# A hybrid attention block on one core: which column groups start with one k-tile, and when normalised queries and keys are scaled

## The chip, the cores and the metric

The kernel runs on one core of a Trainium2 chip. The metric is the time of one execution in microseconds of device time; 574.02 us is the median of three runs of the kernel before. The profile and its trace come from one further execution.

## What is computed

One decoder layer on x of 256 x 2048 in float32:

```python
mod = silu(c) @ w_ada + b_ada                  # 2048 -> 6144: shift, scale, gate
h = rms_norm(x, g_norm) * (1 + scale) + shift
proj = h @ w_in                                # 2048 -> 9296: q, k, v, z of groups a and b, and an indexer
# group a: 8 heads of 128, keys chosen by the indexer's 64 best scores; group b: 8 heads, causal
# q and k of each head are rms-normed; scores get ALiBi; y = attention * silu(z)
out = x + gate * (concat(ya, yb) @ w_out)      # 2048 -> 2048
```

## The kernel before

**Tiles.** `h` is kept transposed, as 16 k-tiles of 128 rows by 256 tokens. w_in has 19 column groups: q, k, v and z of the four quads b0, b1, a0, a1 (512 columns each, four heads), and three indexer groups i0, i1, i2. Float32 accuracy comes from splitting: ScalarE rounds a weight piece to `wh` (L322), VectorE subtracts to get `wl` (L332), and TensorE makes three matmuls for each k-tile and token half (L774 to L776). A *piece* is at most two k-tiles of one group, so 12 matmuls. There are 192 pieces, of which 160 belong to w_in.

**Loads.** All weights come through one in-order queue (SyncE), issued six loads ahead of the casts. w_ada is read transposed in 1 MB loads, two for each k-tile (shift `sh`, scale `sc`); VectorE reduces each against silu(c) (L289, called a *gemv* here). When both loads of the k-tiles of a chunk are reduced, `build_h` makes the h of that chunk (L402 to L418). Chunk 0 is k-tile 0, chunk 1 is k-tile 1, then chunks of two. A planner written in Python lists the loads. It walks the column groups in a fixed order and gives each as many k-tiles as are known then; `between()` inserts w_ada loads by the count of k-tiles listed so far. Where only k-tile 0 is known, the four groups z, q, k, v of a quad are loaded as one quad load of four pieces with one k-tile each. In the kernel before, the list begins: sh0, half of sc0, quad b1, the rest of sc0, then sh1, sc1, sh2, sc2 at once, then quad a0 (again k-tile 0 alone), za1 with k-tiles 0 and 1, sh3, qa1, ka1, va1, sc3, the indexer groups, and so on. Raw weights lie in a pool of four buffers; w_ada loads named by `EARLY` lie in a pool of two (`rawe`). A load waits in the queue until its buffer is free.

**Accumulation.** A group accumulates its listed k-tiles in PSUM; then an evacuation copies (L675) or adds (L677) the sum into SBUF. There are 55 evacuations of w_in groups.

**Attention beside the projections.** Python generators put out the attention work one step at a time, one step after each piece. `yield n` makes a generator skip n steps. `prep` takes the squares of a finished q or k group on ScalarE (L506), gets 1/rms on GpSimd in two instructions (`rsqrt`, L149 and L150), and after `yield 1` scales the eight 128 x 128 blocks on ScalarE (L513). The indexer runs in eight pairs: TensorE transposes q (`ptq`, L466), ScalarE copies it (`qi`, L468), TensorE makes logits (`lg`, L474 and L475), ScalarE applies relu (L477), VectorE adds to the scores (L479). A head transposes q and k (L531), scales k by `gneg` (L534), has GpSimd multiply the distances by the head's slope into `nb` (L536), makes scores (L540, L541), and VectorE adds `nb` and takes the extreme (L545); exp, transposes, value matmuls and the gate follow. The final order of groups is i2, i0, i1, then z, q, k, v of b0, b1, a0, a1. A piece of w_out that needs a head not yet put out forces that head's steps at once.

**Order on the engines.** A scheduler at build time orders each engine's instructions: among those that are ready by its own estimate of times it takes the one that was put out first. On the chip each engine follows that order.

Of the kernel before, what the change touches and what calls it, by code (L numbers as in the profile page):

```python
# [8 lines left out]
F32 = mybir.dt.float32  # L9
F32R = mybir.dt.float32r  # L10
AF = mybir.ActivationFunctionType
ALU = mybir.AluOpType

P = 128
L = 256
D = 2048
KT = D // P
DIN = 9296
HD = 128
# [19 lines left out]
CHUNKS = list(zip(EDGES, EDGES[1:]))  # L39
NC = len(CHUNKS)  # L40


ADA_AT, ADA_FIRST, ADA_GAP, ADA_LAG, GATE_AT, GATE_GAP = 4, 4, 5.5, 2, 150, 8


EARLY = {1, 2} | set(range(5, 2 * KT + KT * KT))


NO_WAIT = mybir.DependencyInfo(mybir.DependencyClass.NoSync, mybir.DependencyReason.DATA)
# [3 lines left out]
def hybrid_block(ctx: ExitStack, tc: tile.TileContext, x, cols, w_ada_t, w_in, w_out, out):  # L53
    nc = tc.nc
    consts = ctx.enter_context(tc.tile_pool(name="consts", bufs=1))
    hp = ctx.enter_context(tc.tile_pool(name="hp", bufs=27))
    up = ctx.enter_context(tc.tile_pool(name="up", bufs=37))
    rawp = ctx.enter_context(tc.tile_pool(name="rawp", bufs=4))
# [4 lines left out]
    rawe = early.enter_context(tc.tile_pool(name="rawe", bufs=2))  # L63
    late_pool = []

    def late_tiles():
        if not late_pool:
            early.close()
            late_pool.append(ctx.enter_context(tc.tile_pool(name="late", bufs=2)))
        return late_pool[0]  # L70
# [9 lines left out]
    def mm_tile(name):  # L80
        return psum.tile([P, 512], F32, tag="mm", bufs=4, name=name)
# [18 lines left out]
    cc = consts.tile([P, 85], F32, name="cc")  # L100
# [10 lines left out]
    dist = consts.tile([P, 384], F32, name="dist")  # L111
# [7 lines left out]
    dista = consts.tile([P, 384], F32, name="dista")  # L119
# [10 lines left out]
    for n in range(4):  # L130
        pt = mm_tile(f"pts{n}")
# [5 lines left out]
    for k0, k1 in CHUNKS:  # L137
        one = bmod[:, k0 + k1:2 * k1]
        nc.gpsimd.tensor_scalar(one, one, 1.0, None, op0=ALU.add)
    gneg = {}  # L140
    for i, g in enumerate("ab"):
        gt = consts.tile([P, 1], F32, name=f"gneg{g}")
        nc.vector.scalar_tensor_tensor(gt, cc[:, 64 + 2 * i:65 + 2 * i], -(HD ** -0.5),
                                       cc[:, 65 + 2 * i:66 + 2 * i], op0=ALU.mult, op1=ALU.mult)
        gneg[g] = gt

    def rsqrt(dst, ssq, n):
# [26 lines left out]
    ada = [ld for c in range(1, NC) for ld in ada_loads(c)]  # L174
# [2 lines left out]
        gates[4 * n + 3]["end"] = NC + n  # L177
    known, ready = CHUNKS[0][1], []
    pos = {g: 0 for g in ORDER}
    n_kt, ada_at, gate_at = 0, ADA_AT, GATE_AT  # L180

    def between():

        nonlocal ada_at, gate_at
        if ada and n_kt >= ada_at:
            for _ in range(ADA_FIRST if ada_at == ADA_AT else 1):
                ld = ada.pop(0)
                loads.append(ld)
                if "end" in ld:
                    ready.append((n_kt + ADA_LAG, CHUNKS[ld["end"]][1]))  # L190
            ada_at += ADA_GAP
        elif gates and n_kt >= gate_at:
            loads.append(gates.pop(0))
            gate_at += GATE_GAP

    turn = list(ORDER)
    while turn:
        while ready and (ready[0][0] <= n_kt or known == pos[turn[0]]):
            known = ready.pop(0)[1]
            if known == KT:  # L200
                turn.sort(key=FINAL.index)
        g = turn.pop(0)
        c0, w = COLS[g]
        seg0, end = pos[g], known
        assert end > seg0
        gs = [c + g[1:] for c in "zqkv"]
        if g[0] == "z" and end == seg0 + 1 and [pos[o] for o in gs] == 4 * [seg0]:

            between()
            turn = [o for o in turn if o not in gs]  # L210
            members = [w_load(w_in_r, o, COLS[o][0], 512, [seg0], "h", True, True, seg0 == 0, end == KT)
                       for o in gs]
            loads.append(dict(kind="quad", quad=g[1:], k=seg0, members=members))
            n_kt += 4
            for o in gs:
                pos[o] = end
                if end < KT:
                    turn.append(o)
            continue
        for k in range(seg0, end, 4):  # L220
            n = min(4, end - k)
            between()
            loads.append(w_load(w_in_r, g, c0, w, list(range(k, k + n)), "h", k == seg0, k + n == end,
                                seg0 == 0, end == KT))
            n_kt += n * w / 512
        pos[g] = end
        if end < KT:
            turn.append(g)
# [9 lines left out]
    n_start = 2 * CHUNKS[0][1] + 1  # L238
    loads.insert(n_start - 1, loads.pop(n_start))
    n_issued = 0  # L240
    late = []

    def issue(upto):
        nonlocal n_issued
        while n_issued < min(upto, len(loads)):
            ld = loads[n_issued]

            pool = rawe if ld["kind"] == "ada" and ld["to"][0] == "mod" and n_issued - n_start in EARLY else rawp
            raw = pool.tile([P, 2048], F32, tag="raw", name=f"raw{n_issued}")
            if ld["kind"] == "ada":  # L250
                h0, h1 = ld["h"]
                ld["v"] = raw[:, :h1 - h0]
                nc.sync.dma_start(ld["v"], w_ada_t[ld["col"] * P:(ld["col"] + 1) * P, h0:h1])
                while late:
                    nc.sync.dma_start(*late.pop(0))
            elif ld["kind"] == "quad":

                q, k = ld["quad"], ld["k"]
                base, off = 0 if q[0] == "a" else COLS["qb0"][0], 512 * int(q[1])
                v = raw.rearrange("p (c n) -> p c n", n=512)  # L260
                src = w_in[k * P:(k + 1) * P, base:base + 4096].rearrange("p (c n) -> p c n", n=1024)
                first_c = (COLS[ld["members"][0]["g"]][0] - base - off) // 1024
                if n_issued == n_start - 1:

                    nc.sync.dma_start(v[:, first_c:first_c + 1, :], src[:, first_c:first_c + 1, off:off + 512])
                    rest = [(lo, hi) for lo, hi in ((first_c + 1, 4), (0, first_c)) if hi > lo]
                    late.extend((v[:, lo:hi, :], src[:, lo:hi, off:off + 512]) for lo, hi in rest)
                else:
                    nc.sync.dma_start(v, src[:, :, off:off + 512])
                for m in ld["members"]:  # L270
                    c = (COLS[m["g"]][0] - base - off) // 1024
                    m["v"] = v[:, c:c + 1, :]
            else:
                kts, w = ld["kts"], ld["w"]
                v = raw[:, :len(kts) * w].rearrange("p (k n) -> p k n", n=w)
                nc.sync.dma_start(v, ld["src"][:, kts[0]:kts[-1] + 1, ld["c0"]:ld["c0"] + w])
                ld["v"] = v
            n_issued += 1

    mod = {}  # L280
# [219 lines left out]
    def prep(q, c):  # L500

        ssq = quad.setdefault((q, c), work.tile([P, 16], F32, name=f"ss{c}{q}", tag="ss", bufs=3))
        for t in range(2):
            for h in range(4):
                junk = work.tile([P, P], F32, name=f"j{c}{q}{t}{h}", tag="junk")
                nc.scalar.activation(junk, proj[c + q, t][:, h * HD:(h + 1) * HD], AF.Square,  # L506
                                     accum_out=ssq[:, 4 * t + h:4 * t + h + 1])
        rsqrt(ssq[:, 8:16], ssq[:, 0:8], HD)
        yield 1
        for t in range(2):  # L510
            for h in range(4):
                s = proj[c + q, t][:, h * HD:(h + 1) * HD]
                nc.scalar.activation(s, s, AF.Copy, scale=ssq[:, 8 + 4 * t + h:9 + 4 * t + h])  # L513
        yield 0
# [9 lines left out]
    def head(q, h):  # L524
        hs = slice(h * HD, (h + 1) * HD)
        hid = int(q[1]) * 4 + h
        name = f"{q}{h}"
        pt = ps_tile("tr", "tr" + name)
        for i, c in enumerate("qk"):
            for t in range(2):  # L530
                nc.tensor.transpose(pt[:, i * L + t * P:i * L + (t + 1) * P], proj[c + q, t][:, hs], ident)  # L531
        qk = late_tiles().tile([P, 512], F32, name="qk" + name, tag="qk", bufs=2)
        nc.vector.tensor_copy(qk[:, :L], pt[:, :L])
        nc.scalar.activation(qk[:, L:], pt[:, L:], AF.Copy, scale=gneg[q[0]])  # L534
        nb = late_tiles().tile([P, 384], F32, name="nb" + name, tag="nb", bufs=2)
        nc.gpsimd.tensor_scalar(nb, dista if q[0] == "a" else dist, 2.0 ** -(hid + 1), 0.0,  # L536
                                op0=ALU.mult, op1=ALU.add)
        yield 1
        ps = ps_tile("s", "s" + name)
        nc.tensor.matmul(ps[:, :P], qk[:, :P], qk[:, L:L + P], start=True, stop=True)  # L540
        nc.tensor.matmul(ps[:, P:384], qk[:, P:L], qk[:, L:], start=True, stop=True)  # L541
        ns = late_tiles().tile([P, 384], F32, name="ns" + name, tag="at", bufs=4)
        st = work.tile([P, 8], F32, name="st" + name, tag="st", bufs=4)
        for t, lo, hi in ((0, 0, P), (1, P, 384)):
            nc.vector.tensor_tensor_reduce(out=ns[:, lo:hi], in0=ps[:, lo:hi], in1=nb[:, lo:hi], scale=1.0,  # L545
                                           scalar=3e38, op0=ALU.add, op1=ALU.min, accum_out=st[:, t:t + 1])
        for t, lo, hi in ((0, 0, P), (1, P, 384)):
            nc.scalar.activation(ns[:, lo:hi], ns[:, lo:hi], AF.Exp, bias=st[:, t:t + 1], scale=-1.0,
# [174 lines left out]
    for j in range(total):  # L723
        sb = subs[j]
        ld = sb["ld"]
# [25 lines left out]
        g = ld["g"]  # L751
# [13 lines left out]
        for i, k, t in order:  # L765
            ps = acc_ps[g, t][:, :w]
# [51 lines left out]
```

## Time and profile before

| | us |
|---|---|
| median of 3 runs | 574.02 (574.01 to 574.69) |
| profiled execution, its own time | 578.7 |
| span of the profiled execution (first to last instruction) | 576.9 |
| TensorE busy | 553.6 (96% of the span) |
| VectorE busy | 444.5 (77%) |
| ScalarE busy | 319.6 (55%) |
| GpSimd busy | 48.0 (8%) |
| mean granted TensorE clock | 0.995 of full speed |

Ends of matmuls are modelled, so busy TensorE time hides short gaps; the distance between starts of consecutive matmuls shows them.

### The profile page before, as it was taken

What the parts mean: (1) busy time and instruction counts of PE and PEld (TensorE: products, weight loads), DVE (VectorE), ACT (ScalarE), POOL (GpSimd) and SP (SyncE); (2) the same over time, 40 slices, a digit from 0 to 9 for tenths busy, and PEclk for the clock granted to TensorE, in tenths of its full rate; (3) what the DMA queues carried; (4) which work ended last, traced back from release to release, by engine and by line L of the source; (5) the groups of instructions that cost most, each with busy time, mean ns of one, the idle gap of its engine ahead of it and who ended that gap; (6) DMA issues with size and microseconds to landing.
All of it is one profiled execution on the core that took longest, in us unless ns stands there. A gap on an engine that the chain in (4) does not pass through costs nothing.

```text
span 576.9 us, 7456 instructions
## 1 busy us (share of the span) xinstructions
PE 553.6 (96%) x2658; PEld 462.7 (80%) x2658; DVE 444.5 (77%) x683; ACT 319.6 (55%) x652; POOL 48.0 (8%) x62
## 2 busy tenths in 40 slices
PE   3889999999999999999799999999999999999996
PEld 2769888888889988976577888888888888887885
DVE  4877789898898898998689996678787576458452
ACT  4588563544444353576555566646776785554340
POOL 4100000000000000102201002111110210000000
PEclk9999999999999999999989999999999999999999
DMA  8999998898898987877845376767675468445611
GB/s 293 412 350 370 361 346 326 330 360 285 314 359 318 366 326 270 268 298 279 303 152 177 129 275 235 273 221 265 226 255 201 148 231 279 146 150 190 244 37 38
DMA packets 59670, 150.09 MB, mean 260 GB/s; under 512 B 3056, under 2 KB 9456, under 8 KB 53616
## 3 DMA queue, kind: packets, MB, share of 16 engines
q1 hardware_dynamic: 58480, 147.51, 71.1%
q10 hardware_dynamic: 1152, 2.10, 1.2%
q8 instruction: 21, 0.34, 0.2%
q14 instruction: 17, 0.14, 0.1%
HBM read 147.50 MB, written 2.10 MB: 259 GB/s over the span
## 4 chain that ended last, share of the span: by engine, by line
PE 87%; ACT 4%; DVE 2%; POOL 2%; issue 2%; DMA 1%; SPq 0%; DVEq 0%; ACTq 0%
PE mm_y_o L774 5%; PE mm_y_o L776 5%; PE mm_y_o L775 5%; PE mm_h_zb L776 3%; PE mm_h_zb L774 3%; PE mm_h_zb L775 3%; PE mm_h_za L775 3%; PE mm_h_i L776 3%; PE mm_h_i L775 3%; PE mm_h_i L774 3%; PE mm_h_qb L774 3%; PE mm_h_za L776 3%; PE mm_h_qb L776 3%; PE mm_h_qb L775 3%; PE mm_h_qa L774 3%; PE mm_h_ka L775 2%
## 5 line engine op out<-in xcount | busy, mean ns | idle before, releaser
L322 ACT ACTIVATE wh<-raw 128x1024 fp32r<-128x1024 f32 (+3 forms) x192 | 188.2, 990 | 140.5 <-PE mm_y_o L776 32.9
L332 DVE TENSOR_TENSOR wl<-raw,wh 128x1024 fp32r<-128x1024 f32 (+3 forms) x192 | 215.0, 1140 | 60.5 <-ACT wh L322 59.9
L289 DVE CUSTOM_DVE_ANT_0 raw<-raw,s_row 128x2048 f32<-128x2048 f32 (+1 forms) x49 | 110.2, 2250 | 14.1 <-DMA raw<-in_w_ada_t 14.1
L774 PE MATMUL mm_y_o<-wh,yT 128*128 128x512 f32 x128 | 51.7, 404 | 0.0
L775 PE MATMUL mm_y_o<-wl,yT 128*128 128x512 f32 x128 | 49.9, 390 | 0.0
L776 PE MATMUL mm_y_o<-wh,yT 128*128 128x512 f32 x128 | 49.8, 390 | 0.0
L774 PE MATMUL mm_h_i<-wh,hhi 128*128 128x384 f32 (+1 forms) x96 | 31.7, 330 | 0.0
L775 PE MATMUL mm_h_i<-wl,hhi 128*128 128x384 f32 (+1 forms) x96 | 31.5, 328 | 0.0
L536 POOL TENSOR_SCALAR nbb<-dist 128x384 f32<-128x384 f32 x8 | 8.0, 1001 | 283.3 <-DVE mmod L289 211.2
L776 PE MATMUL mm_h_i<-wh,hlo 128*128 128x384 f32 (+1 forms) x96 | 31.4, 329 | 0.0
L776 PEld LDWEIGHTS mm_y_o<-wh,yT 128*128 128x128 f32 x128 | 24.0, 188 | 5.4 <-DVE yT L575 0.2
L774 PEld LDWEIGHTS mm_y_o<-wh,yT 128*128 128x128 f32 x128 | 24.1, 188 | 4.7 <-ACT yT L574 0.2
L775 PEld LDWEIGHTS mm_y_o<-wl,yT 128*128 128x128 f32 x128 | 24.1, 188 | 4.6
L774 PE MATMUL mm_h_qa<-wh,hhi 128*128 128x512 f32 x64 | 25.6, 409 | 0.9 <-ACT wh L322 0.9
L774 PE MATMUL mm_h_zb<-wh,hhi 128*128 128x512 f32 x64 | 26.4, 412 | 0.0
L774 PE MATMUL mm_h_vb<-wh,hhi 128*128 128x512 f32 x64 | 26.4, 412 | 0.0
L775 PE MATMUL mm_h_za<-wl,hhi 128*128 128x512 f32 x64 | 25.1, 392 | 0.9 <-DVE wl L332 0.9
L774 PE MATMUL mm_h_kb<-wh,hhi 128*128 128x512 f32 x64 | 25.7, 405 | 0.0
L775 PE MATMUL mm_h_zb<-wl,hhi 128*128 128x512 f32 x64 | 25.7, 401 | 0.0
L775 PE MATMUL mm_h_vb<-wl,hhi 128*128 128x512 f32 x64 | 25.6, 400 | 0.0
L774 PE MATMUL mm_h_qb<-wh,hhi 128*128 128x512 f32 x64 | 25.5, 401 | 0.0
L774 PE MATMUL mm_h_za<-wh,hhi 128*128 128x512 f32 x64 | 25.5, 406 | 0.0
(216 smaller groups left out, 1227.3 us busy)
## 6 DMA issues: line engine op xcount, KB each, us to landing
raw<-in_w_in SPq DMA_DIRECT2D x51, 1024.0 KB, 5.9
raw<-in_w_ada_t SPq DMA_DIRECT2D x47, 1024.0 KB, 6.2
raw<-in_w_out SPq DMA_DIRECT2D x16, 1024.0 KB, 5.0
raw<-in_w_in SPq DMA_DIRECT2D x17, 512.0 KB, 3.6
raw<-in_w_in SPq DMA_DIRECT2D x11, 768.0 KB, 4.6
x<-in_x SPq DMA_DIRECT2D x8, 256.0 KB, 6.9
xr<-in_x ACTq DMA_DIRECT2D x8, 256.0 KB, 6.5
raw<-in_w_in SPq DMA_DIRECT2D x3, 672.0 KB, 7.4
```

The lines of the kernel that those rows point to most:

```text
L289: nc.vector.tensor_tensor_reduce(out=ld["v"], in0=ld["v"], in1=s_row[:, h0:h1], scale=1.0, scalar=0.0, op0=ALU.mult, op1=ALU.add, accum_ou ...
L322: nc.scalar.activation(hi[:, :n, :w], v, AF.Copy)
L332: nc.vector.tensor_tensor(lo[:, :n, :w], v, sb["hi"][:, :n, :w].bitcast(F32), op=ALU.subtract)
L536: nc.gpsimd.tensor_scalar(nb, dista if q[0] == "a" else dist, 2.0 ** -(hid + 1), 0.0, op0=ALU.mult, op1=ALU.add)
L774: nc.tensor.matmul(ps, a_hi, sb["hi"][:, i, :w], start=st, stop=False)
L775: nc.tensor.matmul(ps, a_hi, sb["lo"][:, i, :w], start=False, stop=False)
L776: nc.tensor.matmul(ps, a_lo, sb["hi"][:, i, :w], start=False, stop=en)
```

## The change

- The quad form (one k-tile, four groups in one load) is left to the first quad, b1. The planner now offers the w_ada loads before it takes the next group, so that with sh1 and sc1 listed chunk 1 counts as known at once. All other groups start with two k-tiles or more. The list begins: sh0, half of sc0, quad b1, the rest of sc0, sh1, sc1, za0 with k-tiles 0 and 1, sh2, qa0, sc2, ka0, sh3, va0, za1, qa1, sc3, ka1, and from va1 on four k-tiles.
- All w_ada loads for h after the first chunk lie in `rawe`, its two buffers in turn.
- In all there are 188 pieces in place of 192, 54 evacuations in place of 55, and 157 loads in place of 156. The final order of groups is as before, but the groups have other k-tiles left then: qb0 and kb0 have twelve each (two and twelve before).
- `prep` skips two steps between squares and scaling in place of one.
- GpSimd no longer makes `nb`. The slope goes into the reduction L545 as its `scale`, which reads `dist` or `dista` itself; `gneg` becomes a 128 x 8 tile that has the inverse slope multiplied in. GpSimd makes it at the start from eight memsets and one multiply for each group; the two VectorE instructions L143 go.

```diff
-ADA_AT, ADA_FIRST, ADA_GAP, ADA_LAG, GATE_AT, GATE_GAP = 4, 4, 5.5, 2, 150, 8
-EARLY = {1, 2} | set(range(5, 2 * KT + KT * KT))
+ADA_FIRST, ADA_GAP, ADA_LAG, GATE_AT, GATE_GAP = (4, 4, 6, 8, 10, 15), 5.5, 2, 150, 8
...
+    steep = consts.tile([P, 8], F32, name="steep")
+    for h in range(8):
+        nc.gpsimd.memset(steep[:, h:h + 1], -(HD ** -0.5) * 2.0 ** (h + 1))
     for i, g in enumerate("ab"):
-        gt = consts.tile([P, 1], F32, name=f"gneg{g}")
-        nc.vector.scalar_tensor_tensor(gt, cc[:, 64 + 2 * i:65 + 2 * i], -(HD ** -0.5),
-                                       cc[:, 65 + 2 * i:66 + 2 * i], op0=ALU.mult, op1=ALU.mult)
+        gt = consts.tile([P, 8], F32, name=f"gneg{g}")
+        nc.gpsimd.tensor_scalar(gt, steep, cc[:, 64 + 2 * i:65 + 2 * i], cc[:, 65 + 2 * i:66 + 2 * i],
+                                op0=ALU.mult, op1=ALU.mult)
...
-        if ada and n_kt >= ada_at:
-            for _ in range(ADA_FIRST if ada_at == ADA_AT else 1):
+        if ada and n_kt >= ada_at[0]:
+            at = ada_at[0]
+            while ada and ada_at[0] == at:
                 ld = ada.pop(0)
                 loads.append(ld)
                 if "end" in ld:
-                    ready.append((n_kt + ADA_LAG, CHUNKS[ld["end"]][1]))
-            ada_at += ADA_GAP
+                    ready.append((n_kt + (ADA_LAG if ld["end"] > 1 else 0), CHUNKS[ld["end"]][1]))
+                if ada:
+                    ada_at.pop(0)
...
     while turn:
+        if n_kt and known == CHUNKS[0][1] and not ready:
+            between()
         while ready and (ready[0][0] <= n_kt or known == pos[turn[0]]):
...
-            pool = rawe if ld["kind"] == "ada" and ld["to"][0] == "mod" and n_issued - n_start in EARLY else rawp
+            pool = rawe if ld["kind"] == "ada" and ld["to"][0] == "mod" and n_issued > n_start else rawp
...
         rsqrt(ssq[:, 8:16], ssq[:, 0:8], HD)
-        yield 1
+        yield 2
...
-        nc.scalar.activation(qk[:, L:], pt[:, L:], AF.Copy, scale=gneg[q[0]])
-        nb = late_tiles().tile([P, 384], F32, name="nb" + name, tag="nb", bufs=2)
-        nc.gpsimd.tensor_scalar(nb, dista if q[0] == "a" else dist, 2.0 ** -(hid + 1), 0.0,
-                                op0=ALU.mult, op1=ALU.add)
+        nc.scalar.activation(qk[:, L:], pt[:, L:], AF.Copy, scale=gneg[q[0]][:, hid:hid + 1])
+        far = dista if q[0] == "a" else dist
...
-            nc.vector.tensor_tensor_reduce(out=ns[:, lo:hi], in0=ps[:, lo:hi], in1=nb[:, lo:hi], scale=1.0,
+            nc.vector.tensor_tensor_reduce(out=ns[:, lo:hi], in0=ps[:, lo:hi], in1=far[:, lo:hi],
+                                           scale=2.0 ** -(hid + 1),
```

## Rows read from the trace of the kernel before

**Rows 1.** Waits of the whole run: total us, times, longest us.
```profile
PE lg L474 <- ACT qi L468: 4.4, 2, 3.2
```

**Rows 2.** Windows: length, busy us (instructions) by engine, granted clock, DMA share, GB/s.
```profile
42.00:235.00 193.00, 192.90 (x909) 165.60 (x908) 166.09 (x192) 96.51 (x130) 0.99 (x2) 1.00 0.90 331
...
288.00:292.00 4.00, 4.00 (x14) 3.10 (x12) 3.07 (x5) 2.59 (x4) 0.00 (x0) 0.57 0.02 6
```

**Rows 3.** Chain that ended last, near 25 us: start us, us, what.
```profile
22.86 0.23 PE mm_h_qb L774
...
26.52 0.89 PE ptx L373 x8
```

**Rows 4.** Timeline, 28 to 41 us: start us, us, what [idle before <-releaser].
```profile
28.62 1.95 PE L373 MATMUL ptx<-diag,x 128*128 128x128 f32 x16
...
30.73 2.28 DVE L289 CUSTOM_DVE_ANT_0 raw<-raw,s_row 128x2048 f32<-128x2048 f32 x1
...
32.94 2.49 DVE L332 TENSOR_TENSOR wl<-raw,wh 128x512 fp32r<-128x512 f32 x4
...
33.68 0.51 PE L775 MATMUL mm_h_za<-wl,hhi 128*128 128x512 f32 x1 [0.86 <-DVE wl L332]
...
38.11 1.22 DVE L332 TENSOR_TENSOR wl<-raw,wh 128x1024 fp32r<-128x1024 f32 x1
...
38.58 0.63 PE L774 MATMUL mm_h_za<-wh,hhi 128*128 128x512 f32 x2
...
40.06 0.98 PE L774 MATMUL mm_h_qa<-wh,hhi 128*128 128x512 f32 x2 [0.86 <-ACT wh L322]
...
40.88 0.40 PE L775 MATMUL mm_h_za<-wl,hhi 128*128 128x512 f32 x1
```

**Rows 5.** Timeline of SyncE's queue: the issues of sh1, sc1, sh2, sc2.
```profile
10.85 4.92 SPq L253 DMA_DIRECT2D raw<-in_w_ada_t  x4
```

**Rows 6.** Timeline of VectorE: the gemvs of sh1 and sc1.
```profile
20.80 2.29 DVE L289 CUSTOM_DVE_ANT_0 raw<-raw,s_row 128x2048 f32<-128x2048 f32 x1
...
24.39 2.29 DVE L289 CUSTOM_DVE_ANT_0 raw<-raw,s_row 128x2048 f32<-128x2048 f32 x1
```

**Rows 7.** Timeline of GpSimd, first 20 us.
```profile
2.72 1.78 POOL L139 TENSOR_SCALAR cc<-cc 128x1 f32<-128x1 f32 x9 [0.59 <-DMA cc<-in_cols]
...
11.24 0.19 POOL L149 TENSOR_SCALAR rx<-rx 128x1 f32<-128x1 f32 x1 [5.54 <-DVE rx L358]
```

**Rows 8.** Timeline, 280 to 287 us: kb0's 1/rms and scaling.
```profile
280.17 0.38 PE L466 MATMUL ptq<-ident,p_i 128*128 128x128 f32 x2
...
281.26 3.94 POOL L150 TENSOR_TENSOR sskb<-sskb,mhalf 128x8 f32<-128x8 f32 x1
...
281.43 2.28 DVE L289 CUSTOM_DVE_ANT_0 raw<-raw,s_row 128x2048 f32<-128x2048 f32 x1
...
285.24 0.98 ACT L513 ACTIVATE p_kb<-p_kb,sskb 128x128 f32<-128x128 f32 x3 [4.39 <-POOL sskb L150]
286.13 0.36 ACT L468 ACTIVATE qi<-ptq 128x256 f32<-128x256 f32 x1
...
286.54 0.50 PE L474 MATMUL lg<-kiT,qi 64*128 64x128 f32 x4 [3.24 <-ACT qi L468]
```

**Rows 9.** Timeline, 262 to 270 us: qb0's scaling and the logits after it.
```profile
262.71 2.45 ACT L513 ACTIVATE p_qb<-p_qb,ssqb 128x128 f32<-128x128 f32 x8 [3.02 <-POOL ssqb L150]
...
269.07 0.50 PE L474 MATMUL lg<-kiT,qi 64*128 64x128 f32 x4 [1.13 <-ACT qi L468]
```

**Rows 10.** Instructions of L150: ns min/median/max, first and last start.
```profile
L150 POOL TENSOR_TENSOR ssqa<-ssqa,mhalf x2: 1635/1635/1635, 409.8 to 456.4; 128x8 f32<-128x8 f32 x2
```

**Rows 11.** Timeline of GpSimd: the first two multiplications of distances.
```profile
227.63 0.99 POOL L536 TENSOR_SCALAR nbb<-dist 128x384 f32<-128x384 f32 x2 [211.18 <-DVE mmod L289]
```

**Rows 12.** Timeline, 514 to 522 us: the last head's score and value matmuls.
```profile
514.79 0.38 PE L540 MATMUL sa<-qka 128*128 128x128 f32 x2
...
521.23 0.67 PE L563 MATMUL pva<-pTa,p_va 128*128 128x256 f32 x2
```

More of the change, by code (lines that the diff above doesn't have):

```diff
@@ L179, in hybrid_block @@
     pos = {g: 0 for g in ORDER}
-    n_kt, ada_at, gate_at = 0, ADA_AT, GATE_AT
+    n_kt, gate_at = 0, GATE_AT
+    ada_at = list(ADA_FIRST)
+    ada_at += [ADA_FIRST[-1] + ADA_GAP * (i + 1) for i in range(len(ada) - len(ada_at))]
     def between():
-        nonlocal ada_at, gate_at
-        if ada and n_kt >= ada_at:
-            for _ in range(ADA_FIRST if ada_at == ADA_AT else 1):
+        nonlocal gate_at
+        if ada and n_kt >= ada_at[0]:
+            at = ada_at[0]
+            while ada and ada_at[0] == at:
                 ld = ada.pop(0)
```

## The prediction

> **What bounds the kernel now.** TensorE is busy 96% of the span, so I read first where it is not fed: the list of waits, then windows by stage, then the timeline of each stage with a gap. Between 42 and 235 us TensorE is busy 192.9 of 193.0 us [rows 2]: nothing can be won there, and the number of matmuls does not change. The waits name one cause above all, logits that wait for `qi` on ScalarE, 4.4 us in two places [rows 1]. A third place is the start, right after the first quad, where short waits follow each other [rows 4]. A gap is counted by starts: a matmul of 512 columns takes 0.23 us of the chain, eight x transposes 0.89 us [rows 3], a piece of 12 matmuls so 2.76 us.
>
> **The start, what is lost there.** From the 24 transposes at 28.62 us to the first matmul of za1 at 38.58 us pass 9.96 us. The work in between is 24 transposes (3 x 0.89 = 2.67 us) and the 24 matmuls of quad a0 (5.52 us), 8.19 us. Lost: 1.77 us. The next four matmuls take from 38.58 to 40.88 us, 2.30 us for 0.92 us of work: 1.38 us more. Together 3.15 us. The reader is to see who is late [rows 4]: at 33.68 us `wl`, which VectorE begins at 32.94 us, straight after the gemv of 30.73 us. All four early gemvs stand ahead of quad a0's casts. At 40.06 us it is `wh`: four groups with one k-tile need four evacuations in the time of two pieces, and ScalarE falls behind.
>
> **The start, after the change.** za0 follows with only sh1 and sc1 ahead of it. Its `wl` can come right after sc1's gemv, which ends at 24.39 + 2.29 = 26.7 us [rows 6], so at 27.9 us with the 1.22 us of a whole piece [rows 4]. qa0, ka0 and va0 then cost VectorE a gemv and a `wl` each, 2.29 + 1.22 = 3.51 us: ready at 31.4, 34.9 and 38.4 us. TensorE is through the transposes at 28.62 + 2.67 = 31.3 us and wants the pieces at 31.3, 34.1, 36.8 and 39.6 us. VectorE's lead shrinks from 2.7 us (qa0) to 1.2 us (va0), less about 0.7 us for the h of chunk 1, but it stays. After va0 come two pieces with no gemv ahead. One evacuation comes per 2.76 us in place of two, which takes ScalarE's lateness away.
>
> Moved past SyncE's queue are sh2 and sc2, and all that is queued behind them. Before, four issues were through at 10.85 + 4.92 = 15.8 us [rows 5]. Now sh2 waits for one of two buffers, until sh1's gemv ends at 23.1 us [rows 6], with qa0, sc2, ka0 and sh3 queued behind. sc2 waits for sc1's gemv (26.7 us). The slack is what covers this: qa0 is wanted on TensorE at 34.1 us, 11 us after its issue. If the cover were gone, each late piece would cost up to 3.51 - 2.76 = 0.75 us, 2.25 us for three. So the gain here lies between 3.15 us (nothing lost any more) and 3.15 - 2.25 = 0.9 us; if the loads themselves come late it is nothing. I take 2.05 us, with 1.1 us still lost to the wait for transposes' buffers and to a late va0.
>
> Four casts fewer and one evacuation fewer: two half-wide `wl` cost 1.24 us (half of 2.49 us), a whole one 1.22 us [rows 4]; so nothing, and what evacuations cost is hidden beside matmuls.
>
> **1/rms and scaling: what is lost.** The reader is to follow kb0 [rows 8]. GpSimd begins L150 at 281.26 us and takes 3.94 us. ScalarE has the scaling L513 next and stands 4.39 us. Behind it stands `qi` of the next pair, whose transposes were made at 280.17 us; it runs at 286.13 us and the logits begin 3.24 us late. TensorE's clock is then 0.57 of full speed from 288 to 292 us [rows 2], the lower level for most of the stretch: 4.0 x 0.43 = 1.7 us more. For qb0 ScalarE stands 3.02 us, then scales for 2.45 us; the backlog makes the logits 1.13 us late [rows 9]. Sum: 3.24 + 1.7 + 1.13 = 6.1 us.
>
> Why is L150 so long? Undisturbed it takes 1.64 us [rows 10]; here a gemv of 2.28 us begins 0.17 us after it [rows 8], and 1.64 + 2.28 = 3.92 us.
>
> The Trainium skill, SBUF — State Buffer, section Who interferes with whom, says that a VectorE instruction with two SBUF inputs and a GpSimd instruction that reads SBUF exclude each other, and that the earlier one goes first. The trace agrees on the exclusion (3.94 us against 1.64 us), not on the order: the gemv, shown later, kept its 2.28 us. By that rule the length of the stop hangs on whether a gate's gemv falls on L150, and not on the skipped step.
>
> **After the change.** Two things move. The extra skipped step puts one more weight cast ahead of the scalings where both are ready. It does not hold the scalings back by itself: the scheduler takes what is ready, as the first `nb` shows, done at 227.63 us [rows 11], long before qb0 was even scaled at 262.71 us [rows 9]. Second, the phase of pairs against `prep` changes. Before, kb0's squares go out with the logits of one pair, and the next `qi` one piece later, so its transposes come when L150 starts. Now a `qi` goes out ahead of the squares of qb0 and of kb0, and the next one two pieces later. In kb0's case the transposes would come a piece later, at 280.17 + 2.76 = 282.9 us, and the logits be wanted after one more piece, at 285.7 us and a little. ScalarE is free of the stop at 285.2 us. If `qi` is then first, nothing is lost; if all eight scalings stand ahead (2.45 us [rows 9]) it is about 2 us late. I take the middle, 1.0 us for each of qb0 and kb0, and no drop of the clock, as none followed the 1.13 us wait. Left: 2.0 us; gain 4.1 us. The ends: both stops vanish (gain 6.1 us), or both become like kb0's, 2 x (3.24 + 1.7) = 9.9 us, a loss of 3.8 us.
>
> **Work taken from GpSimd.** The sixteen multiplications (two took 0.99 us [rows 11]) run long before they are needed; taking them away gives nothing. L545 keeps its form; its scale was 1.0. At the start eight memsets and two multiplies come to GpSimd. The nearest row is nine small ones in 1.78 us, so 2.0 us for ten, and GpSimd then stands idle 5.54 us before the 1/rms of x [rows 7]. Nothing; without that cover 2.0 us, as the 1/rms of x starts the first transposes.
>
> **The tail.** Later scaling and fewer pieces between ka1 and the w_out pieces that need a1's heads (15 in place of 16, and the scaling a piece later) press the last heads. Before, the last head took 521.23 - 514.79 = 6.44 us from scores to values [rows 12], with pieces in between to hide it. With a piece less, up to 2.76 us can come bare. The other pieces of w_out can fill most of it: I take 0.5 us, between 0 and 2.76.
>
> **The sum.** -2.05 (start) - 4.1 (scaling) + 0.5 (tail) = -5.65 us. On the profiled execution, 578.7 us, that gives 573.0 us. The median of the runs is 4.7 us lower, 574.02 us, and I move it by the same: 568.4 us.
>
> **The rivals.**
> - *The stops stay as they are.* The skipped step changes only who goes first, and GpSimd's lengths stay. For it: `nb` ran as soon as it could [rows 11]. Against: the new phase of the pairs. Time: 574.02 - 2.05 + 0.5 = 572.5 us.
> - *The start gains nothing*, because sh2 and all behind it wait for `rawe`. For it: issue at 23.1 us in place of at most 15.8 us. Against: 11 us of slack. Time: 574.02 - 4.1 + 0.5 = 570.4 us.
> - *All stops vanish.* If no gemv falls on L150 the 1/rms takes 1.64 us, 2.3 us less than kb0's, and ScalarE's stop of 4.39 us is halved. Time: 574.02 - 3.15 - 6.1 = 564.8 us. The skill's rule above speaks for this one as much as for the first rival.
> - *Slower.* In the stretch of qb0 and kb0 both `prep` now meet the pairs in one phase, so a bad phase comes twice: ScalarE stands behind L150 in both, TensorE stops 3.24 us and loses 1.7 us of clock each time. Time: 574.02 - 2.05 + 3.8 + 0.5 = 576.3 us. It decides from where the two stops, clock included, cost more than 6.1 + 2.05 - 0.5 = 7.7 us.
>
> **How the numbers follow.** Forecast 0.47, with a range of its own from 566 to 571; the stops stay 0.20; no gain at the start 0.08; all vanish 0.13; slower 0.12. The range reaches from below the case in which all vanishes, 564.0, to 574.5, above the stops that stay, and leaves out most of the slower case and tails: about 0.18. 0.2% is 1.15 us (572.87 to 575.17), about what a measurement of this kernel can tell from no change. Faster: 0.46 + 0.11 of the stops that stay (572.5 is just below the bound) + 0.08 + 0.13 = 0.78, say 0.77. Same: 0.07 of the stops that stay, the rest of the others, 0.11. Slower: 0.12.
>
> **What the profile would show.** Start: za0 begins within 1 us of the transposes' end, and no wait of TensorE for `wl` or `wh` over 0.5 us up to va1. Scaling: waits of logits for `qi` at 2 us or less in all, and the granted clock at 1.00 beside vb0. Tail: TensorE without a gap over 0.5 us near the last head. The prediction is wrong if the list of waits still shows 3 us or more for `qi`, or if a new wait stands between 42 and 235 us.

## The result, and the profile after

The changed kernel takes 581.02 us (median of five, 580.91 to 581.45). The kernel before takes 574.69 us (median of five beside it); the ratio is 1.0103, 95% interval 1.0079 to 1.0127. So it is slower by 1%, where I had forecast faster by 1%, and it lies above my range (564.0 to 574.5 us). The profiled execution after took 580.91 us (span 579.1 us), near its median. The profiled execution before took 578.7 us, one of the longer ones: beside the first experiments 3 of 25 runs of before took 577 us or more, over all four rounds of experiments 24 of 105.

The list of waits of TensorE after, against [rows 1]:

```profile
PE mm_h_ka L782 <- ACT wh L330: 1.6, 1, 1.6
PE ptk L465 <- ACT kk L460: 1.0, 1, 1.0
PE mm_h_vb L783 <- DVE wl L340: 0.9, 2, 0.5
PE mm_h_va L783 <- DVE wl L340: 0.8, 2, 0.5
PE lg L482 <- ACT qi L476: 0.6, 1, 0.6
PE mm_h_ka L783 <- DVE wl L340: 0.5, 1, 0.5
PE mm_h_qa L783 <- DVE wl L340: 0.4, 1, 0.4
PE mm_h_vb L782 <- ACT wh L330: 0.3, 1, 0.3
```

The wait for `qi`, 4.4 us before, is down to 0.6 us, as forecast. In its place stand waits for casts, `wh` and `wl`, of the pieces at the start (34 to 57 us) and of vb0 and vb1 at 90 to 122 us. The indexer's transposes `ptk` wait 1.0 us for `kk` (0.2 us before); I had not expected that either, and no run here is about it. The windows, with the columns of [rows 2]:

```profile
40.00:44.00 4.00, 4.00 (x11) 3.04 (x11) 2.50 (x3) 1.57 (x3) 0.00 (x0) 0.57 1.03 408
...
80.00:130.00 50.00, 48.81 (x213) 39.18 (x212) 40.30 (x49) 25.72 (x34) 0.00 (x0) 1.00 0.86 324
...
288.00:292.00 4.00, 4.00 (x22) 2.85 (x22) 3.71 (x4) 4.00 (x19) 1.51 (x2) 1.00 0.41 112
```

The drop of the clock to 0.57 at 288 us is gone, but there is one at 40 us. It follows a stop of TensorE, which the timeline of TensorE and ScalarE shows (start us, us, what, idle before and its releaser):

```profile
35.79 0.60 ACT L683 ACTIVATE p_qa<-mm_h_qa 128x512 f32<-128x512 f32 x1 [2.29 <-PE mm_h_qa L784]
36.92 0.60 ACT L683 ACTIVATE p_qa<-mm_h_qa 128x512 f32<-128x512 f32 x1 [0.54 <-PE mm_h_qa L784]
37.42 1.05 ACT L330 ACTIVATE wh<-raw 128x1024 fp32r<-128x1024 f32 x1
...
38.52 0.73 PE L782 MATMUL mm_h_ka<-wh,hhi 128*128 128x512 f32 x2 [1.63 <-ACT wh L330]
39.78 0.50 PE L783 MATMUL mm_h_ka<-wl,hhi 128*128 128x512 f32 x1 [0.53 <-DVE wl L340]
...
40.77 0.63 PE L783 MATMUL mm_h_ka<-wl,hhi 128*128 128x512 f32 x1
41.19 0.63 PE L784 MATMUL mm_h_ka<-wh,hlo 128*128 128x512 f32 x1
```

The reader is to see ScalarE, not TensorE, in the first row: it stands idle 2.29 us and then does the evacuation of qa0, whose end TensorE has to reach first. Only behind both evacuations comes ka0's `wh`. So TensorE finishes qa0, waits for an evacuation and a cast, and only then can begin ka0: 1.63 + 0.53 us. From 40.36 us matmuls begin 0.42 us apart in place of 0.23 us for about 3 us, the lower level of the clock (0.57 over the 4 us window).

To see how much each stretch loses I add up, over consecutive matmuls, the distance of their starts less the usual distance for that width (0.227 us for 512 columns, the same for all kernels); it is worked out from the traces, good to about 0.1 us. "Before again" is the first experiment below.

```
us lost in               20:60   80:140   240:320   480:540   whole run
before, first profile      4.4      0       10.6       0.8       30.4
before again (e1)          4.0      0        6.8       0.9       27.0
after                      6.9      2.3      5.9       1.7       32.0
```

Against an ordinary execution of before, the change loses 2.9 us at the start, 2.3 us at 80 to 140 us and 0.8 us at the tail, and wins 0.9 us at the scalings: 5.1 us, of the 6.3 us between the medians.

### The profile page after: what moved, and what is told of

Read it like the earlier page. It is cut to its first block, busy times and chain, and to the rows that moved or that the text cites. A ratio compares the mean times of both kernels' runs of the same rounds, so it can differ in the third digit from the quotient of the medians.

```text
span 579.1 us, 7420 instructions
## 1 busy us (share of the span) xinstructions
PE 555.6 (96%) x2658; PEld 461.6 (80%) x2658; DVE 442.3 (76%) x675; ACT 317.8 (55%) x648; POOL 27.2 (5%) x56
## 4 chain that ended last, share of the span: by engine, by line
PE 89%; ACT 4%; DVE 3%; issue 1%; DMA 1%; POOL 1%; SPq 0%; DVEq 0%; ACTq 0%
PE mm_y_o L782 5%; PE mm_y_o L784 5%; PE mm_y_o L783 5%; PE mm_h_va L783 3%; PE mm_h_vb L783 3%; PE mm_h_va L784 3%; PE mm_h_zb L782 3%; PE mm_h_i L782 3%; PE mm_h_za L782 3%; PE mm_h_i L784 2%; PE mm_h_i L783 2%; PE mm_h_zb L783 2%; PE mm_h_za L783 2%; PE mm_h_za L784 2%; PE mm_h_vb L784 2%; PE mm_h_zb L784 2%
## 5 line engine op out<-in xcount | busy, mean ns | idle before, releaser
L782 PE MATMUL mm_h_i<-wh,hhi 128*128 128x384 f32 (+1 forms) x96 | 31.4, 329 | 0.0
L782 PE MATMUL mm_h_ka<-wh,hhi 128*128 128x512 f32 x64 | 25.9, 412 | 1.6 <-ACT wh L330 1.6
L783 PE MATMUL mm_h_ka<-wl,hhi 128*128 128x512 f32 x64 | 25.8, 403 | 0.5 <-DVE wl L340 0.5
L783 PE MATMUL mm_h_va<-wl,hhi 128*128 128x512 f32 x64 | 25.3, 395 | 0.9 <-DVE wl L340 0.8
L784 PE MATMUL mm_h_ka<-wh,hlo 128*128 128x512 f32 x64 | 25.7, 401 | 0.0
```

Source lines behind the costliest of these rows:

```text
L782: nc.tensor.matmul(ps, a_hi, sb["hi"][:, i, :w], start=st, stop=False)
L783: nc.tensor.matmul(ps, a_hi, sb["lo"][:, i, :w], start=False, stop=False)
L784: nc.tensor.matmul(ps, a_lo, sb["hi"][:, i, :w], start=False, stop=en)
```

## The experiments

Three questions led the runs. Which part of the change costs: the new order of loads and pieces (theory A) or the rest (rival C)? If it is the order, do the casts come late because they stand behind evacuations (A2) or because loads come late (A1)? And were the stops that I counted in my sum there in an ordinary execution? The letters of the expectations belong to each run; A in the first run is not A in the second.

**Before again.** No edit.

> The kernel before, unchanged, profiled once more. Theory A (my prediction's sum was sound, but made against an execution 4.7 us longer than the others): this execution's span is near 572 us, and the rows show no granted clock of 0.57 at 288:292 and waits of logits for qi of at most 2 us in place of 4.4 us; then the 4.1 us that I counted as a gain at the scalings were mostly not there to be won. Rival B: the stops stand in every execution, the span is near 577 us or the waits are the same 4.4 us, and the 4.7 us lie somewhere else. Time against the kernel before: the same within 0.2%.

575.43 us, ratio 1.0007 (0.9983 to 1.0031); its profile is of an execution of 575.22 us, span 573.4 us. Its waits, windows (262 to 292 us) and the stop at kb0, against [rows 1, 2, 8]:

```profile
PE lg L474 <- ACT qi L468: 2.2, 2, 1.1
```

```profile
262.00:288.00 26.00, 23.79 (x121) 17.80 (x118) 20.51 (x29) 18.89 (x51) 2.94 (x3) 1.00 0.87 313
288.00:292.00 4.00, 4.00 (x25) 3.04 (x23) 3.84 (x7) 2.38 (x5) 0.00 (x0) 1.00 0.40 140
```

```profile
280.40 1.40 DVE L479 SCALAR_TENSOR_TENSOR sc<-rl,w,sc 128x128 f32<-128x128 f32 x4
281.89 2.29 DVE L289 CUSTOM_DVE_ANT_0 raw<-raw,s_row 128x2048 f32<-128x2048 f32 x1
...
281.55 1.75 POOL L150 TENSOR_TENSOR sskb<-sskb,mhalf 128x8 f32<-128x8 f32 x1
...
283.33 0.99 ACT L513 ACTIVATE p_kb<-p_kb,sskb 128x128 f32<-128x128 f32 x3 [2.19 <-POOL sskb L150]
```

Theory A of this run holds, though by a little less than written (span 573.4 us where I had said near 572 us, waits of 2.2 us where I had said at most 2 us). The same program, with the same order on each engine, has L150 at 1.75 us in place of 3.94 us, the wait for `qi` behind it at 1.1 in place of 3.2 us, and no drop of the clock. What differs is a fraction of a microsecond: here the gemv begins 0.34 us after L150, in [rows 8] 0.17 us after it.

**Only the plan, only the rest.** The new order of loads, first pieces and buffers alone; and the later scaling, the fused slope and the slopes on GpSimd alone.

> Only the changed order of loads and first pieces (four groups with one k-tile, w_ada loads one by one, all early w_ada loads through the two rawe buffers); the scalings one step later, the fused distance bias and the table of slopes are left as before. Theory A (the start is what costs): 577 to 580 us, slower than before by 3 to 6 us, with TensorE's wait for ka0's wh and the granted clock of about 0.57 at 40:44 in its rows. Rival C (the skipped step or the work moved to GpSimd costs): 573 to 575 us, and the rest alone is slower.

> Only the rest: scalings of queries and keys one step later, distance bias fused, slopes on GpSimd; loads and first pieces as before. Theory A (the start is what costs, the rest gains a little): 570 to 574 us. My prediction's step for this part was -4.1 us and +0.5 us at the tail, so 571. Rival C: 576 us or more.

The plan alone: 580.97 us, 1.0098 (1.0064 to 1.0132). The rest alone: 576.04 us beside 575.46, 1.0012 (0.9986 to 1.0037). The whole loss is the plan's, as theory A has it. Two things came out otherwise. The rest alone gains nothing: A had 570 to 574 us, and 576.04 us lies by its number in rival C's range, though it can't be told from before beside it. And the plan alone, with the same two waits for ka0 (1.6 and 0.5 us), keeps the full clock at 40 us, where I had expected 0.57:

```profile
40.00:44.00 4.00, 3.17 (x12) 2.10 (x12) 3.12 (x4) 2.18 (x4) 0.00 (x0) 1.00 1.04 413
```

It is as slow as the changed kernel all the same, and by the sum of the first table it loses 6.7 us at 20:60 (6.9 us after). So the drop of the clock comes with the stop, and not always; it is not what makes the kernel slow.

Against my sum stand the waits for `qi`, first of the plan alone, then of the rest alone:

```profile
PE lg L478 <- ACT qi L472: 0.6, 1, 0.6
```

```profile
PE lg L478 <- ACT qi L472: 2.4, 1, 2.4
```

The plan takes the wait away without the skipped step, and the skipped step does not take it away without the plan. Of the plan it is the pieces that do it: in the two runs on its halves below, the waits are 0.6 us with the new pieces and 2.1 us with the old ones.

**Buffers and order.** Two edits to the changed kernel, each alone and both together. In the first the instructions of every engine stand in the same order as after; in the second ScalarE's order differs only around four casts, wh of qa0, ka0, va0 and vb0, and one matmul of za0 stands two places earlier on TensorE.

```diff
-... and n_issued > n_start else rawp
+... and n_issued > n_start and n_issued not in (7, 9) else rawp
```

Loads 7 and 9 are sh2 and sc2; they go to the weights' four buffers.

> The changed kernel, with sh2 and sc2 in the weights' buffers as before in place of the two rawe buffers; each engine's instructions stand in the same order. Theory A1 (the loads wait for the two buffers, and data comes late): ka0's wh and the pieces after it come earlier, the wait of 1.6 us at 38.5 us and the clock drop at 40:44 go, 577 to 579 us, 2 to 4 us faster than the changed kernel. Rival A2 (ScalarE's order is what holds ka0's wh back, behind two evacuations, and not the data): the wait stays within 0.3 us of 1.6 us and the time within 1 us of 581.0 us.

```diff
-        sb["hi"] = hi
+        sb["hi"], sb["cast"] = hi, nc.cur_bb.bb.instructions[-1]
...
+            n = len(nc.cur_bb.bb.instructions)
             evac(ld)
+            if ld["kset"] == "h" and ld["start"] and 4 <= j:
+                for ins in nc.cur_bb.bb.instructions[n:]:
+                    if ins.engine == subs[j + 1]["cast"].engine:
+                        tc.add_manual_dep(ins, subs[j + 1]["cast"].name, NO_WAIT, reason="cast first")
```

> The changed kernel with one thing added: where a group's first evacuation runs on ScalarE, it stands behind the wh of the next piece, where the changed kernel has it ahead (four places: the wh of qa0, ka0, va0 and vb0). Loads, buffers and sizes are as in the changed kernel. Theory A2 (ScalarE's order holds the casts back although their data landed 3 us or more before): the 1.6 us and 0.5 us waits for ka0's wh and wl and the granted clock of 0.57 at 40:44 go, and the waits at 90 us too; 577 to 578 us, 3 to 4 us faster than the changed kernel. Rival A3 (the casts come too late anyway, by VectorE's gemvs or the number of wide casts, and another wait takes the place): 580 to 581.5 us.

> Two of the experiments together on the changed kernel: the casts ahead of the evacuations, and sh2 and sc2 in the weights' buffers. Theory A2: as with the casts alone within 0.8 us, since landings are not what the casts wait for: 576 to 578 us. Rival A1 (with the casts moved up, the landings become the next limit): 2 us or more faster than with the casts alone.

Buffers alone: 580.18 us, 1.0078 (1.005 to 1.0106), the wait for ka0's `wh` still 1.6 us. Casts first alone: 576.58 us, 1.0023 (1.0009 to 1.0038). Both: 575.04 us, 0.9987 (0.9969 to 1.0006). ScalarE with casts first:

```profile
34.21 1.06 ACT L330 ACTIVATE wh<-raw 128x1024 fp32r<-128x1024 f32 x1
36.36 0.60 ACT L683 ACTIVATE p_qa<-mm_h_qa 128x512 f32<-128x512 f32 x1 [1.08 <-PE mm_h_qa L784]
37.50 0.60 ACT L683 ACTIVATE p_qa<-mm_h_qa 128x512 f32<-128x512 f32 x1 [0.54 <-PE mm_h_qa L784]
39.93 1.06 ACT L330 ACTIVATE wh<-raw 128x1024 fp32r<-128x1024 f32 x1 [1.83 <-DMA raw<-in_w_in]
```

ka0's `wh` runs at 34.21 us, 3.2 us earlier than after, so its data was there. The next cast, va0's, now waits for its load: this is where the buffers begin to count. They are worth 1.5 us (576.58 - 575.04, one round) once the casts stand first. While the casts stand behind evacuations nothing can be told: 0.8 us (581.02 - 580.18) lies between two rounds in which before itself moved as much (574.69 and 575.46 us), and TensorE loses 7.0 us at 20:60 with them, 6.9 us without. The order is worth 4.4 us (581.02 - 576.58; 4.6 us if each is taken by its ratio to before). A2 is the main cause and A1 the second; both together gain 1.5 us over the casts alone, between the 0.8 us that A2 allowed and the 2 us that A1 asked for. The sum of losses is 26.3 us with both (2.8 us at 20:60, 0.9 us at 80:140).

**Which half of the plan.** The block of four w_ada loads as before with the new pieces; and the old pieces with w_ada spread between them. Each edit moves the buffers too: in the block sh2 and sc2 (there loads 6 and 7) lie in the weights' buffers, as before; with the spread all early w_ada loads share the two `rawe` buffers, as after.

```diff
-ADA_FIRST, ADA_GAP, ... = (4, 4, 6, 8, 10, 15), 5.5, ...
+ADA_FIRST, ADA_GAP, ... = (4, 4, 4, 4, 10, 15), 5.5, ...
...
-... and n_issued > n_start else rawp
+... and n_issued > n_start and n_issued not in (6, 7) else rawp
```

```diff
-ADA_AT, ADA_FIRST, ADA_GAP, ... = 4, 4, 5.5, ...
+ADA_AT, ADA_GAP, ... = (4, 4, 8, 10, 12, 15), 5.5, ...
...
-        if ada and n_kt >= ada_at:
-            for _ in range(ADA_FIRST if ada_at == ADA_AT else 1):
+        if ada and n_kt >= ada_at[0]:
+            for _ in range(2 if n_kt == 4 else 1):
+                ada_at.pop(0)
...
-... and n_issued - n_start in EARLY else rawp
+... and n_issued > n_start else rawp
```

> The changed kernel, but its first four w_ada loads (sh1, sc1, sh2, sc2) stand in one block ahead of za0, as before; the first pieces are those of the change (four groups with one k-tile, the others with two). Theory D (the spread of w_ada between the pieces is what costs): 575 to 577 us. Theory E (the new first pieces cost, each with an evacuation of its own and a whole cast behind it): 579 to 582 us.

> The kernel before with its eight groups of one k-tile, but with w_ada spread as in the change: sh1 and sc1 ahead of quad a0, then sh2, sc2, sh3, sc3 one by one between the pieces, all through the two rawe buffers. Theory D (the spread costs): 578 to 581 us. Theory E (the new first pieces cost): 574 to 576 us, no slower than before.

Block with new pieces: 577.11 us, 1.0025 (1.0011 to 1.004). Old pieces with spread: 579.16 us, 1.0065 (1.004 to 1.0089), its times far apart (577.04 to 586.36). Theory D holds: the spread, its buffers included, costs 3.9 us with the new pieces (581.02 - 577.11) and 3.8 us with the old (579.16 - 575.35). With sh2 and sc2 in the weights' buffers on both sides it is 3.1 us (580.18 - 577.11). The block lies 0.1 us outside its range and is still 1.8 us slower than before (577.11 - 575.35): that is the share of theory E, the pieces. TensorE's losses tell the two apart. The block loses 4.1 us at 20:60, as before does, and as much as after at 80:140; the old pieces with spread lose 6.5 us at 20:60 and nothing at 80:140. So the spread makes the loss at the start, and the new pieces make the one at vb0 and vb1. ScalarE in the block, and then in the old pieces with spread:

```profile
30.43 2.01 ACT L330 ACTIVATE wh<-raw 128x1024 fp32r<-128x1024 f32 x2
33.34 1.06 ACT L330 ACTIVATE wh<-raw 128x1024 fp32r<-128x1024 f32 x1 [0.91 <-DMA raw<-in_w_in]
35.34 0.60 ACT L683 ACTIVATE p_za<-mm_h_za 128x512 f32<-128x512 f32 x1 [0.94 <-PE mm_h_za L784]
```

```profile
42.16 0.60 ACT L676 ACTIVATE p_qa<-mm_h_qa 128x512 f32<-128x512 f32 x1 [2.29 <-PE mm_h_qa L777]
43.29 0.60 ACT L676 ACTIVATE p_qa<-mm_h_qa 128x512 f32<-128x512 f32 x1 [0.54 <-PE mm_h_qa L777]
43.79 2.00 ACT L323 ACTIVATE wh<-raw 128x1024 fp32r<-128x1024 f32 x2
```

With the block, three casts stand ahead of za0's evacuation; with the spread, the same stop as after appears one quad later, at 42 us, behind old pieces. At the start it is the spread that makes the order put casts behind evacuations. Why the scheduler does so (its estimate of when the loads land is the likeliest) was not tried.

**One load later.** Both cures, with sh3 behind va0.

> The experiment with both cures (casts ahead of evacuations, sh2 and sc2 in the weights' buffers), with one load moved: sh3 one piece later, behind va0. Theory A2/A1 (with the casts moved up, the landing of va0 behind sh3 is what the start still waits for): the wait of 0.5 us for va0's wl at 39.8 us goes and so may the one at 51.3 us; 573.9 to 575 us. Rival: the wait moves to a later piece, behind sc3, and the time stays at 575.0 within 0.5 us.

575.11 us, 0.9983 (0.9963 to 1.0003). The waits for `wl` in va went, and those in ka grew from 0.3 to 1.3 us: the rival holds.

**What the scalings are worth.** The kernel before without the 1/rms of queries and keys (L149 and L150 of `prep`, with a constant as the scale).

> The kernel before, with the 1/rms of queries and keys left out (GpSimd's L149 and L150 of each prep; the squares stay, and the scalings multiply by a constant). ScalarE's scalings then wait for nothing but their data. This bounds what the stops at the scalings are worth. My prediction's term (6.1 us lost there): 568 to 570.5 us. Rival T4 (an ordinary execution loses 2.2 us there, and has no drop of the clock): 572.5 to 574.5 us.

572.32 us, 0.9936 (0.9912 to 0.9959), 2.8 us less than before beside it (575.09 us). No wait for `qi` is left. That is 0.2 us below T4's range and 1.8 us above that of my term: between the medians GpSimd's 1/rms costs 2.8 us, not 6.1 us. In the first profile of before, though, 6.1 us was read rightly: the run without 1/rms loses 4.5 us at 240:320, 6.1 us less than that profile (10.6 us) and 2.3 us less than before again (6.8 us). The times say the same: of the 26 runs of before beside this one 9 took 577 us or more, and without 1/rms all nine lie between 571.59 and 572.99 us. That the stop at kb0 makes all the longer ones was read from one trace of them alone.

**The skipped step.** Casts first and the buffers ("both cures") with `yield 1` again; two further profiled executions of that kernel; then one step for the b quads or the a quads alone.

> The experiment with both cures (casts ahead of evacuations, sh2 and sc2 in the weights' buffers), with the scalings back at one skipped step as in the kernel before. My prediction's step (the extra skipped step moves the scalings out of the way of qi): logits wait for qi by 2 us or more again, 577 us or more. Rival (the shape of the first pieces sets where the scalings fall among the pairs, and the skipped step does nothing): waits for qi stay at 0.6 us, 574.5 to 575.5 us.

> One look at the kernel of the run with one skipped step and both cures, whose twelve times fell into two groups, 575.4 to 576.6 and 578.2 to 579.8 us; the profile read so far was of the first. Theory P (a 1/rms on GpSimd and a work of VectorE that starts within some 0.2 us of it decide by chance, as in kb0's stop): a profile of the second group shows one L152 of 2.5 us or more where the first has 1.64 us, and TensorE's stop behind it, 2 us or more with the clock. Rival Q (the whole execution is slower, by the granted clock or by transfers): the waits are the same and the loss is spread.

> A second look at the same kernel as in the first look (one skipped step, both cures), since one profile falls in either group. Theory P: as there, one long L152 and the stop behind it in an execution over 578 us, none in one under 577 us. Rival Q: no single stop.

> Both cures, with one skipped step for the scalings of quads b0 and b1 and two for a0 and a1. If the second group comes from the b quads (the stops that my prediction spoke of): twelve times spread over 3 us or more, median 576 us or more. If it comes from the a quads: within 1.5 us of each other, median near 575 us.

> Both cures, with one skipped step for the scalings of quads a0 and a1 and two for b0 and b1. If the second group comes from the a quads (late heads, beside the last pieces of w_in): spread of 3 us or more, median 576 us or more. If from the b quads: within 1.5 us, median near 575 us.

One step: 577.38 us, 1.0031 (1.0007 to 1.0054), the wait for `qi` still 0.6 us: neither side as written. The two further executions: 577.58 and 577.97 us. One step in the b quads: 576.56 us, 1.0022 (0.9996 to 1.0048), seven times up to 576.8, one of 577.7 and four from 578.5 to 579.8 us; in the a quads: 576.48 us, 1.0005 (0.998 to 1.003), eleven of twelve up to 577.05 and one of 579.16 us. By the words of the two expectations both halves would be the cause (each over 576 us and spread over more than 3 us), so these two runs do not part them. The profiles show one stop, and only with one step in the b quads: a wait that the changed kernel does not have. Waits between 338 and 370 us, and TensorE's, first with one step (575.73 us), then one step in the b quads (an execution of 579.66 us):

```profile
DVE raw L297 <- DMA raw<-in_w_ada_t: 1.2, 1, 1.2
...
PE trb L539 <- ACT gate L438: 0.7, 1, 0.7
```

```profile
DVE raw L297 <- DMA raw<-in_w_ada_t: 2.9, 1, 2.9
...
PE trb L539 <- ACT gate L438: 2.2, 1, 2.2
```

The two further executions have 2.2 and 1.7 us, 2.1 and 1.6 us; the plan alone, which has one step too, 0.7 and 0.2 us. In all five TensorE waits 0.5 to 0.7 us less than VectorE waited for its load. By the sum of the first table TensorE loses 1.3, 3.2, 2.8 and 4.6 us at 340:400 in the four with both cures (one step, its two further executions, one step in the b quads), and 0.5 us with two steps or with one step in the a quads; most of what their spans differ by (573.9, 575.8, 576.2, 577.9 us) lies there. The rows between, of the first of these kernels (575.73 us), give the chain:

```profile
353.22 2.29 DVE L297 CUSTOM_DVE_ANT_0 raw<-raw,s_row 128x2048 f32<-128x2048 f32 x1 [1.16 <-DMA raw<-in_w_ada_t]
...
355.43 0.69 DVE L685 TENSOR_TENSOR p_qb<-mm_h_qb,p_qb 128x512 f32<-128x512 f32 x1
...
375.72 2.45 ACT L521 ACTIVATE p_kb<-p_kb,sskb 128x128 f32<-128x128 f32 x8 [1.09 <-POOL sskb L152]
378.08 2.00 ACT L330 ACTIVATE wh<-raw 128x1024 fp32r<-128x1024 f32 x2
379.98 0.57 ACT L438 ACTIVATE gate<-pgate 128x512 f32<-128x512 f32 x1
```

A gemv waits for its load; q's evacuation, the squares, the scalings, two casts and a gate stand behind it, and TensorE's transposes of the first b0 head (L539) behind the gate. After a stop of 2.2 us the clock fell to 0.64 at 384:388. So Theory P's place was wrong (L152 took 1.64 or 1.65 us in all), Rival Q as well: the landing of one load, different in every execution, is what goes with the stop. No run moved that load alone, so this is read from five profiles and not tested. With two steps no such wait stands in the profile with both cures, and TensorE never waits there. Why one step in the a quads has a median of 576.48 us stays open: its profiled execution took 574.95 us, the shortest of the twelve.

## Why the prediction was wrong, point by point

**The start (-2.05 us forecast, about +5.2 us).** The step that failed is "One evacuation comes per 2.76 us in place of two, which takes ScalarE's lateness away", with "nothing" as the price of what ScalarE does. I costed VectorE's instructions and the loads' slack, and never asked in which order ScalarE's evacuations and casts stand. For ka0 the slack was there: it was on the chip 3 us before it was cast. But a cast behind the evacuation of the piece before it can't begin until TensorE has finished that piece, so each such piece costs a hand-over, for ka0 1.63 + 0.53 us. Putting the casts first gave 4.4 us of the 6.3 us back. I had looked for a wait of SyncE; undoing that alone (the rival of 570.4 us) gave nothing that can be told from noise, and 1.5 us once the casts stood first. The same order came back at 90 us (vb0), by the new pieces, where I had expected nothing to be lost; a new wait between 42 and 235 us was one of the signs that I had named for being wrong. The one rival that had forecast a slower kernel (576.3 us) rested on the scalings, and they did not get worse.

**What I said of `wl`.** za0's `wl` was forecast for 27.9 us and ended at 29.9 us, though VectorE was through sc1's gemv at 25.9 us, earlier than forecast: it stood idle 2.37 us for ScalarE's `wh`; those of qa0, ka0 and va0 for 31.4, 34.9 and 38.4 us, and they ended at 34.3, 39.7 and 44.7 us. The error grows from 2.0 to 6.3 us over the four pieces, as a hand-over each time would make it.

**The scalings (-4.1 us forecast).** In the profiles the stop went as forecast: 4.4 to 0.6 us of waits, the clock at 1.00, and against the execution that I had read TensorE loses 4.7 us less at 240:320 (10.6 and 5.9 us). Two things were wrong. The size: 6.1 us was one execution's loss. The one nearer the median loses 2.2 us to `qi`, and 2.8 us is all that could be had between medians; moving the gain from an execution 4.7 us above the median onto the median counted the same stop twice. The cause: the pieces change the phase, not the skipped step (0.6 us with the new pieces and one step). That the forecast of the wait came true is luck as far as the skipped step goes. The skipped step does win, but elsewhere: 2.3 us between the medians with one step and two (577.38 and 575.04 us, of different rounds). One part of it is the stop at b0's first head; the part of the a quads was not found.

**The tail (+0.5 us forecast).** The sum of losses at 480:540 rose by 0.8 us: right in sign and near in size. The plan alone has 1.5 us there and the rest alone 0.9 us, so it goes with the plan and not with the later scaling. It lies in many short gaps of up to 0.34 us: the last head did not come bare, and that a guess of 0.5 us between 0 and 2.76 us came near is luck.

**GpSimd's work (nothing forecast).** Right: the rest alone is the same as before within its interval. The ten small instructions took 0.97 us, and GpSimd still stood idle 4.72 us before the 1/rms of x.

**L150 and the gemv.** The Trainium skill, SBUF — State Buffer, section Who interferes with whom, says that issue order decides who blocks. The two executions of the same program do not bear that out: the gemv begins after L150 in both, by 0.34 us and by 0.17 us, and keeps its length in both (2.29 and 2.28 us), while L150 takes 1.75 us in the one and 3.94 us in the other. In the rows VectorE's instruction before the gemv ends at 280.40 + 1.40 = 281.80 us in the first, 0.09 us before the gemv begins, and at 280.11 + 1.40 = 281.51 us in the second, after the gemv has begun at 281.43 us. That a gap in VectorE's work let GpSimd in, and that without one the gemv went first, fits these two and was not tested. Two other rows of before limit it, and my reading of 1.64 + 2.28 us with it:

```profile
259.95 2.36 DVE L332 TENSOR_TENSOR wl<-raw,wh 128x1024 fp32r<-128x1024 f32 x2
260.17 2.51 POOL L150 TENSOR_TENSOR ssqb<-ssqb,mhalf 128x8 f32<-128x8 f32 x1
...
361.62 1.64 POOL L150 TENSOR_TENSOR sskb<-sskb,mhalf 128x8 f32<-128x8 f32 x1
362.08 2.29 DVE L289 CUSTOM_DVE_ANT_0 raw<-raw,s_row 128x2048 f32<-128x2048 f32 x1 [1.60 <-DMA raw<-in_w_ada_t]
```

In the first pair two `wl` follow each other without a gap, and L150 takes 2.51 us, where waiting for both would make 262.31 - 260.17 + 1.64 = 3.8 us (an estimate). In the second a gemv runs beside L150 for 1.2 us, and neither grows. So a gemv that falls on L150 does not lengthen it by itself, as I had taken it; the two of [rows 10] that I called undisturbed run beside VectorE too (a gemv begins 0.96 us after the first, a `wl` 0.61 us after the second). What decides stays open.

## What to carry to other kernels

Where loads are moved, look on each engine for what stands between a landed load and its use: a row of ScalarE idle with TensorE as its releaser, followed by an evacuation and then a cast, shows a piece tied to the end of the one before, which no list of transfers shows. A stop read from one execution that lies well above the median belongs to that execution until a second profile shows it too. Undo suspected parts alone and together: the buffers alone gave nothing clear of noise here, the order 4.4 us and both 6.0 us (581.02 - 575.04), so the buffers' share shows only when the order is right.

## What the runs showed that I had not expected

One program ran with L150 at 3.94 us or at 1.75 us, as the gemv began 0.17 us or 0.34 us after it, with 3.5 us of span between the two executions. And one load of w_ada landed earlier or later relative to the same order of work: in three executions of one program VectorE waited 1.2, 2.2 and 2.1 us for it, in one of its sister with one step in the b quads 2.9 us, and TensorE's stop moved along.

No version here that computes the whole result beats the median of the kernel before by more than can be measured: the best two are at 0.9987 (0.9969 to 1.0006) and 0.9983 (0.9963 to 1.0003). They vary less, though: with both cures twelve runs lie between 574.29 and 575.79 us, where 31 of before in the same round lie between 573.81 and 578.91 us.
